# A two-layer diffusion backbone on one core: context-first token groups and a rebuilt entry into the seven-product FFN

## The chip, the cores and the metric

One core of a Trainium2 chip runs the whole network in one launch. The metric is the device time of one execution in microseconds, the median of several runs. Weights come from device memory in every run; nothing is prepared on the device beforehand.

## The reference, cut to what matters

```python
D_MODEL, SEQ, DEPTH, CTX_LEN, D_FF = 1024, 512, 2, 256, 2816

def modulate(t, g, shift, scale):
    return rmsnorm(t, g) * (1.0 + scale) + shift

def ada_mod(cond, w, b):
    m = jax.nn.silu(cond) @ w + b
...
def swiglu(h, w_up, w_down):
    a, b = jnp.split(h @ w_up, 2, axis=-1)
    return (jax.nn.silu(a) * b) @ w_down

def ffn_sublayer(t, mod, i, g, w_up, w_down):
    h = modulate(t, g, mod[3 * i], mod[3 * i + 1])
    return t + 0.5 * mod[3 * i + 2] * swiglu(h, w_up, w_down)
...
def merge_branches(o_a, o_b, g_logits, b_gate, w_pa, w_pb, w_o):
    g_a, g_b = jnp.split(jax.nn.sigmoid(g_logits + b_gate), 2, axis=-1)
    return (g_a * (o_a @ w_pa) + g_b * (o_b @ w_pb)) @ w_o
```

Each of the two layers is a half-step FFN, a token mixing (neighbourhood attention and a gating MLP, merged by gates and projected), and a second half-step FFN. All run over 512 latent and 256 context tokens with the same weights; the second FFN of layer 1 needs the latent tokens alone. Everything is in fp32.

## The kernel before

Activations lie transposed: a tile is 128 channels (partitions) by up to 768 tokens, the latent ones at columns 0 to 511, the context ones at 512 to 767. The residual stream is eight tiles `x`, the input of a stage eight tiles `h`. An fp32 product is made of three fp32r matmuls: every weight and every activation is split into a high part (`hi`, `hh`, `gh`, a rounding cast on ACT) and a remainder (`lo`, `hl`, `gl`, the difference), and PE does hi·hi, hi·lo and lo·hi (L464, L465, L467 for ordinary blocks). One block is 128 output channels: 8 (or fewer) k steps of three matmuls for each token group, gathered in one of eight PSUM banks per group.

**Weights** pass through `Stream` in one fixed order: SP issues the DMA into one of five raw buffers (`wraw`), ACT casts the high part (L253), and GpSimd (POOL) subtracts the remainder (L254); there are nine `wq` tiles for the parts, and a `Unit` of 1024 columns takes two. The raw buffer is free again when the remainder has been made.

**Order.** Tasks are listed up front (`task`), each a generator; while its matmuls are issued, every step advances the weight stream and one step of the background generators (`side`, `side2`, the deferred `tail`). So the order on every engine is fixed when the program is built, and each engine runs its list in order. `extras` puts units of the conditioning product between tasks (ada units: 512 KB raw, two DVE products 128x1024 each, L552); `require` forces those that a stage needs.

**FFN** (`ffn`). The up-projection has 22 pairs of 128 channels (a and b). In the three FFNs that have both token sets (both of layer 0 and the first of layer 1) the first pairs are standard blocks (`up`, and `opening`, which takes the first three blocks one token group after the other), `STANDARD` = four in the very first FFN (the start FFN), two in the later ones. The other pairs go through `up_pair`: seven products of 384 columns (L779 to L781) instead of eight, on sums and differences of quarters of h and of the weights. The operands of h (`t42`, `t3`, `t1`) are made by `combine` from whole h, which POOL restores as hh + hl (tile `hb`, L728), by four subtractions on DVE (L721) and rounding on ACT with a difference on DVE (L746, L747), for each of four k. Then `settle` writes `t1` over the right halves of hh and hl, so no standard block may follow it. `act` makes silu(a)·b for a standard pair (ACT L890, DVE L891) and splits the product into gh (ACT L795) and gl (DVE L796). The quarters of the weights are sums and differences on DVE (L287), with cast and remainder on ACT and DVE. The down-projection runs in parts of four pairs (`MAINS`), between groups of up pairs, with residuals on DVE (L805).

**Between stages.** `close` does the last down (or output) products with the residual, and in its background, for one token group after the other: squares (ACT L619, POOL L626), sums by PE (L635), statistics (L655), the reciprocal root spread over the partitions (L669), and the `norm` of the next stage: per tile `nu` on DVE (L693), hh on ACT (L697), hl on DVE (L706), the latter two with the shift added. Into the later seven-product FFNs the two groups are `EVEN`, 384 and 384 columns.

**Mixing** ends with `gates` (2 x 8 units of 1024), `merge` (8 units of 1024) and `project` (8 of 640), each followed by extras, and then `close`.

## Time and profile before

| | us |
|---|---|
| median of three runs | 3045.46 (3044.94 to 3045.81) |
| profiled execution, its own time | 3043.34 |
| its span in the trace | 3041.5 |
| PE busy | 2919.8 |
| DVE busy | 1804.1 |
| ACT busy | 1112.0 |
| POOL busy | 1069.5 |

The page gives the busy time of each engine over the span. The table of waits says for each engine at which line it stood and what released it. A timeline lists single instructions with start and duration; a bracket gives the idle time in front and what ended it. The granted clock of TensorE is 1.00 or 0.50 of full speed in a short window (2.4 or 1.2 GHz).

### The profile page before, as it was taken

To read this page: it belongs to the slowest core of one execution; us is meant where nothing else is said; L and a number is where in the kernel's file an instruction comes from. 1 tells how busy PE (TensorE), PEld (TensorE's weight loads), DVE (VectorE), ACT (ScalarE), POOL (GpSimd) and SP (SyncE) were. 2 spreads that over 40 slices of the span, in tenths; PEclk is the share of its full clock that TensorE was granted. 3 is DMA by queue.
4 is the path that set the end of the run, shared out by engine and by line. 5 is a ranking of instruction groups with operands and counts; after the bars stand their busy time and mean duration, and the time that the engine had idled before them with its cause. 6 is when DMAs were issued, how large, how long until landed. Compare 5 with 4: busy or idle time off the path is not lost. (4 is left out here: it accounts for less than half of the span.)

```text
span 3041.5 us, 42332 instructions
## 1 busy us (share of the span) xinstructions
PE 2919.8 (96%) x16316; PEld 2652.7 (87%) x16316; DVE 1804.1 (59%) x3075; ACT 1112.0 (37%) x2033; POOL 1069.5 (35%) x760
## 2 busy tenths in 40 slices
PE   8899999999999997999999889999999999999998
PEld 5789999889998887999999789999989887888887
DVE  5787766645566748756766876766564646421113
ACT  4233334334552233334333343333343643332222
POOL 2322222354444343222123422222246545544443
PEclk9899999999999998999999899999999999999999
DMA  6233322242223230322233022333224334332231
GB/s 232 86 114 108 108 91 86 95 153 70 80 87 125 93 113 24 118 86 91 87 111 118 15 75 100 110 122 115 77 93 161 105 101 155 122 97 94 87 97 63
DMA packets 103353, 309.13 MB, mean 102 GB/s; under 512 B 13040, under 2 KB 15344, under 8 KB 103152
## 3 DMA queue, kind: packets, MB, share of 16 engines
q1 hardware_dynamic: 100160, 294.70, 29.2%
q0 software_dynamic: 2560, 11.54, 1.0%
q8 instruction: 128, 2.10, 0.3%
q14 instruction: 73, 0.60, 0.1%
q10 hardware_dynamic: 432, 0.20, 0.0%
HBM read 286.46 MB, written 8.39 MB: 97 GB/s over the span
## 5 line engine op out<-in xcount | busy, mean ns | idle before, releaser
L254 POOL TENSOR_TENSOR wq<-wraw,wq 128x512 fp32r<-128x512 f32 (+2 forms) x454 | 804.9, 1780 | 1645.3 <-ACT wq L253 1379.4
L253 ACT CAST wq<-wraw 128x512 fp32r<-128x512 f32 (+2 forms) x686 | 480.8, 722 | 610.2 <-DMA wraw<-dm 220.7
L464 PE MATMUL ps<-hh,wq 128*128 128x512 f32 (+2 forms) x1344 | 489.3, 364 | 6.1 <-ACT hh L697 6.1
L465 PE MATMUL ps<-hl,wq 128*128 128x512 f32 (+2 forms) x1344 | 470.3, 359 | 1.9 <-DVE hl L706 1.8
L467 PE MATMUL ps<-hh,wq 128*128 128x512 f32 (+2 forms) x1344 | 433.4, 358 | 0.2 <-POOL wq L254 0.2
L464 PE MATMUL ps<-gh,wq 128*128 128x512 f32 (+2 forms) x1248 | 430.8, 345 | 1.9 <-ACT wq L253 1.9
L465 PE MATMUL ps<-gl,wq 128*128 128x512 f32 (+2 forms) x1248 | 406.2, 343 | 0.0
L805 DVE SCALAR_TENSOR_TENSOR x<-ps,mods,x 128x512 f32<-128x512 f32 (+3 forms) x416 | 238.1, 602 | 283.0 <-PE ps L467 282.7
L467 PE MATMUL ps<-gh,wq 128*128 128x512 f32 (+2 forms) x1248 | 350.6, 344 | 0.4 <-POOL wq L254 0.4
L552 DVE SCALAR_TENSOR_TENSOR products<-wraw,condb 128x1024 bf16<-128x1024 f32 x224 | 328.3, 1466 | 2.9 <-DMA wraw<-ada 1.1
L464 PEld LDWEIGHTS ps<-hh,wq 128*128 128x128 f32 x1344 | 256.5, 191 | 56.0 <-ACT hh L697 7.4
L465 PEld LDWEIGHTS ps<-hl,wq 128*128 128x128 f32 x1344 | 256.9, 191 | 38.0 <-DVE hl L706 4.0
L464 PEld LDWEIGHTS ps<-gh,wq 128*128 128x128 f32 x1248 | 235.1, 188 | 54.0 <-ACT wq L253 2.2
L465 PEld LDWEIGHTS ps<-gl,wq 128*128 128x128 f32 x1248 | 235.2, 188 | 28.4
L467 PEld LDWEIGHTS ps<-hh,wq 128*128 128x128 f32 x1344 | 237.3, 192 | 22.7 <-POOL wq L254 0.6
L254 DVE TENSOR_TENSOR wq<-wraw,wq 128x512 fp32r<-128x512 f32 x232 | 179.7, 775 | 64.2 <-ACT wq L253 64.2
L467 PEld LDWEIGHTS ps<-gh,wq 128*128 128x128 f32 x1248 | 202.8, 190 | 8.2 <-POOL wq L254 0.6
L779 PE MATMUL px<-t42h,wq 128*128 128x384 f32 x464 | 159.2, 343 | 14.2 <-ACT ce L908 12.0
L1229 PE MATMUL ps<-wq,hh 128*128 128x256 f32 x704 | 165.2, 329 | 0.0
L779 PE MATMUL pz<-hh,wq 128*128 128x384 f32 x464 | 157.8, 340 | 4.2 <-ACT ce L908 4.2
L781 PE MATMUL px<-t42h,wq 128*128 128x384 f32 x464 | 158.6, 342 | 2.7 <-DVE wq L254 2.7
L780 PE MATMUL px<-t42l,wq 128*128 128x384 f32 x464 | 158.6, 342 | 0.0
(209 smaller groups left out, 5514.9 us busy)
## 6 DMA issues: line engine op xcount, KB each, us to landing
wraw<-up SPq DMA_DIRECT2D x176, 512.0 KB, 3.3
wraw<-ada SPq DMA_DIRECT2D x128, 512.0 KB, 3.3
wraw<-dm SPq DMA_DIRECT2D x160, 256.0 KB, 2.7
wraw<-win SPq DMA_DIRECT2D x72, 512.0 KB, 3.3
wraw<-pab SPq DMA_DIRECT2D x16, 512.0 KB, 3.2
ch<-first SPq DMA_DIRECT2D x16, 384.0 KB, 8.2
xs<-x POOLq DMA_DIRECT2D x16, 384.0 KB, 5.8
bt<-bt SPq DMA_DIRECT2D x16, 384.0 KB, 3.2
```

The source lines that it names most:

```text
L253: self.nc.scalar.copy(out=hi, in_=src)
L254: eng.tensor_tensor(out=lo, in0=src, in1=hi.bitcast(F32), op=ALU.subtract)
L464: nc.tensor.matmul(out[g][:, :n], lhsT=wh, rhs=xh[:, o:o + n], start=first, stop=False)
L465: nc.tensor.matmul(out[g][:, :n], lhsT=wh, rhs=xl[:, o:o + n], start=False, stop=False)
L467: nc.tensor.matmul(out[g][:, :n], lhsT=wl, rhs=xh[:, o:o + n], start=False, stop=last)
L552: nc.vector.scalar_tensor_tensor(out=self.products, in0=unit.raw, scalar=1.0, in1=self.condb[c], op0=ALU.mult, op1=ALU.mult, accum_out=m[: ...
L779: nc.tensor.matmul(ps[:, :H], lhsT=wh, rhs=xh, start=first and k == 0, stop=False, skip_group_check=True)
L780: nc.tensor.matmul(ps[:, :H], lhsT=wh, rhs=xl, start=False, stop=False, skip_group_check=True)
L781: nc.tensor.matmul(ps[:, :H], lhsT=wl, rhs=xh, start=False, stop=last and k == KQ - 1, skip_group_check=True)
L805: self.nc.vector.scalar_tensor_tensor(out=self.x[d][:, o:o + n], in0=ps[:, at:at + n], scalar=self.mod(l, idx, d, p), in1=self.x[d][:, o:o ...
L1229: nc.tensor.matmul(ps[:, at:at + 256], lhsT=c(t[k]), rhs=w, start=k == 0 and i == 0, stop=k == KD - 1 and i == 2)
```

## The change

1. `STANDARD` is (4, 3): the two later seven-product FFNs do three standard pairs instead of two.
2. The token groups at every entry into a seven-product FFN are `BOTH` (context 256, then latent 512) instead of `EVEN`, in `close`, `norm` and `opening`.
3. At those entries `norm` writes into tiles `hb` that are kept: ACT adds the shift a second time in place, so the tile holds whole h, and hl is a plain difference of it and hh. `combine` takes these tiles; POOL's additions are gone. In the start FFN, which has no such norm, the additions are made by DVE, one per step. The settling is part of `combine` now, released by a task behind the last standard block.
4. In the start FFN the first down part stands right behind the four standard pairs, ahead of the first seven-product pair, and has no extras in it.
5. The remainders of the standard up units in the two later seven-product FFNs (12 units of 1024) and of gates (32 units of 1024), merge (16 of 1024) and project (16 of 640) of both layers are made by DVE instead of POOL.
6. Numbers of extras: more in the start's up-products and the rest of that FFN, none in the first half of the gates, more behind merge, some behind project.

```diff
@@ -43,11 +43,11 @@
-EXTRAS = (0.65, 0.65, 0.85, 0)
-MIX_EXTRAS = (1, 0.7)
+EXTRAS = (0.85, 0.65, 0.85, 0)
+MIX_EXTRAS = (1, 1, 1)
 QUIET = 5
-START_EXTRAS = 1.2
-STANDARD = (4, 2)
+START_EXTRAS = 1.6
+STANDARD = (4, 3)
...
-EVEN = ((0, H), (H, H))
...
-            self.split(u.raw[:, :u.n], u.hi, u.lo, self.nc.gpsimd)
+            self.split(u.raw[:, :u.n], u.hi, u.lo, getattr(self.nc, u.eng))
...
-                us[d] = self.t3("nu")[:, :n]
+                if whole is None:
+                    us[d] = self.t3("nu")[:, :n]
+                else:
+                    if len(whole) == d:
+                        whole.append(self.t3("hb"))
+                    us[d] = whole[d][:, o:o + n]
...
+                    if whole is not None:
+                        nc.scalar.activation(
+                            out=us[d][:, at:at + m], in_=us[d][:, at:at + m], func=AF.Identity,
+                            bias=self.mod(l, 3 * i, d, p),
+                        )
...
+                    if whole is not None:
+                        nc.vector.tensor_tensor(
+                            out=hl[e][:, a:a + m], in0=us[e][:, at:at + m], in1=hh[e][:, a:a + m].bitcast(F32),
+                            op=ALU.subtract,
+                        )
+                        continue
...
-    def combine(self, h):
+    def combine(self, h, whole):
...
-                b.append(self.t3("hb"))
-                nc.gpsimd.tensor_tensor(out=b[-1], in0=hh[d].bitcast(F32), in1=hl[d].bitcast(F32), op=ALU.add)
-            yield
+                if whole:
+                    b.append(whole[d])
+                    whole[d] = None
+                else:
+                    b.append(self.t3("hb"))
+                    nc.vector.tensor_tensor(out=b[-1], in0=hh[d].bitcast(F32), in1=hl[d].bitcast(F32), op=ALU.add)
+                    yield
...
+        while not self.may_settle:
+            yield
+        for k in range(KQ):
+            u = t["t1"].pop(0)
+            self.parted(u[:, :H], hh[k][:, H:], hl[k][:, H:])
+            u = None
+            yield
+        self.settled = True
...
-    def settle(self, h):
-
-        while self.side2:
-            self.step()
-        for k, u in enumerate(self.t["t1"]):
-            self.parted(u[:, :H], h[0][k][:, H:], h[1][k][:, H:])
-        self.t["t1"] = None
...
+        eng = "vector" if seven and not start else "gpsimd"
         j0 = STANDARD[not start] if seven else NF
-        ups = [[Unit(A["up"][(base * NF + j) * 2 + s], 1024) for s in range(2)] if j < j0 else
+        ups = [[Unit(A["up"][(base * NF + j) * 2 + s], 1024, eng=eng) for s in range(2)] if j < j0 else
...
-                if j == j0:
-                    self.settle(h)
+                while not self.settled:
+                    self.step()
...
-                if p < len(MAINS) - 1 or d < QUIET:
+                if (p > 0 or not start) and (p < len(MAINS) - 1 or d < QUIET):
                     self.extras(EXTRAS[base])
...
-            while j <= f0 + m if p < len(MAINS) - 1 else j < NF:
+            ahead = f0 + m + (not start or p > 0)
+            while j < ahead if p < len(MAINS) - 1 else j < NF:
                 (up_pair(j) if j >= j0 else up(j)) if j else begin() if start else first()
                 j += 1
+                if j == j0:
+                    self.task([], free)
...
-            for s, un in enumerate((unit(20 + d), unit(28 + d))):
+            for s in range(2):
+                un = Unit(win[20 + 8 * s + d], 1024, eng="vector")
...
-                self.extras(MIX_EXTRAS[0])
+                if d >= KD // 2:
+                    self.extras(MIX_EXTRAS[0])
...
-            un = Unit(A["pab"][l * KD + d], 1024)
+            un = Unit(A["pab"][l * KD + d], 1024, eng="vector")
...
-            un = Unit(A["om"][l * KD + d], (KD - O_LAST) * P)
+            un = Unit(A["om"][l * KD + d], (KD - O_LAST) * P, eng="vector")
...
             self.task([un], gen)
+            self.extras(MIX_EXTRAS[2])
...
-                core.ffn(l, 0, (LAT, CTX), hbox, EVEN, BOTH, box, then(l, 1, BOTH), start=l == 0)
+                core.ffn(l, 0, (LAT, CTX), hbox, BOTH, BOTH, box, then(l, 1, BOTH), start=l == 0)
```

In layer 0 the mixing and the second FFN get their groups in the same way. The order of the instructions moves in three places. In it L717 is the hl of the norm, L739 the subtractions (L721 before), L750 the additions, L780 the differences (L747), L830 the residual (L805), L917 the multiplication (L891), L821 the gl (L796), L253 the remainder (L254), L286 the quarters (L287).

DVE at the entry into the seven products in the second FFN of layer 0, before: the norm's end, the first weight quarters, the combine's first steps.

```order
L706 SCALAR_TENSOR_TENSOR hl<-nu,mods_106,hh 128x256
L287 TENSOR_TENSOR s_10674<-wraw 128x512
L287 TENSOR_TENSOR wraw<-wraw 128x512
L254 TENSOR_TENSOR wq<-wraw,wq 128x512
L287 TENSOR_TENSOR wraw<-wraw 128x512
L721 TENSOR_TENSOR hb<-hb 128x384 x4
L747 TENSOR_TENSOR t42l<-hb,t42h 128x768
L747 TENSOR_TENSOR t3l<-hb,t3h 128x384
L721 TENSOR_TENSOR hb<-hb 128x384 x4
```

DVE at the same place, after: the norm's end, a remainder, the combine's first two steps.

```order
L698 SCALAR_TENSOR_TENSOR hb<-x,mods_106,rs 128x512
L717 TENSOR_TENSOR hl<-hb,hh 128x512 x2
L253 TENSOR_TENSOR wq<-wraw,wq 128x1024
L739 TENSOR_TENSOR hb<-hb 128x384 x4
L780 TENSOR_TENSOR t42l<-hb,t42h 128x768
L780 TENSOR_TENSOR t3l<-hb,t3h 128x384
L739 TENSOR_TENSOR hb<-hb 128x384 x4
L780 TENSOR_TENSOR t42l<-hb,t42h 128x768
```

The quarters of the first seven-product weights have left this place, and one remainder of a whole unit has come. At the combine's end in the kernel before:

```order
L747 TENSOR_TENSOR t42l<-hb,t42h 128x768
L747 TENSOR_TENSOR t3l<-hb,t3h 128x384
L891 TENSOR_TENSOR s<-s,ps 128x384 x2
L796 TENSOR_TENSOR gl<-s,gh 128x768
L254 TENSOR_TENSOR wq<-wraw,wq 128x512 x2
L287 TENSOR_TENSOR wraw<-wraw 128x512
```

And after:

```order
L780 TENSOR_TENSOR t42l<-hb,t42h 128x768
L780 TENSOR_TENSOR t3l<-hb,t3h 128x384
L917 TENSOR_TENSOR s<-s,ps 128x512
L917 TENSOR_TENSOR s<-s,ps 128x256
L821 TENSOR_TENSOR gl<-s,gh 128x768
L253 TENSOR_TENSOR wq<-wraw,wq 128x1024 x2
L286 TENSOR_TENSOR s_10896<-wraw 128x512
L286 TENSOR_TENSOR wraw<-wraw 128x512
```

The remainders behind the first multiplication are those of a standard unit, the quarters come later.

DVE at the transition from the mixing of layer 0 into that FFN, before: residuals of the closing projection (L805), between them pieces of the first group's norm, then the statistics of the second.

```order
L805 SCALAR_TENSOR_TENSOR x<-ps,mods_106,x 128x128
L805 SCALAR_TENSOR_TENSOR x<-ps,mods_106,x 128x256
L693 SCALAR_TENSOR_TENSOR nu<-x,mods_106,rs 128x384
L706 SCALAR_TENSOR_TENSOR hl<-nu,mods_106,hh 128x384
L693 SCALAR_TENSOR_TENSOR nu<-x,mods_106,rs 128x384
L706 SCALAR_TENSOR_TENSOR hl<-nu,mods_106,hh 128x384
L805 SCALAR_TENSOR_TENSOR x<-ps,mods_106,x 128x128
L805 SCALAR_TENSOR_TENSOR x<-ps,mods_106,x 128x256
L693 SCALAR_TENSOR_TENSOR nu<-x,mods_106,rs 128x384
L706 SCALAR_TENSOR_TENSOR hl<-nu,mods_106,hh 128x384 x2
L658 TENSOR_SCALAR nw<-st 128x3
```

And after:

```order
L698 SCALAR_TENSOR_TENSOR hb<-x,mods_106,rs 128x256
L717 TENSOR_TENSOR hl<-hb,hh 128x256
L253 TENSOR_TENSOR wq<-wraw,wq 128x1024
L830 SCALAR_TENSOR_TENSOR x<-ps,mods_106,x 128x512
L698 SCALAR_TENSOR_TENSOR hb<-x,mods_106,rs 128x256
L717 TENSOR_TENSOR hl<-hb,hh 128x256
L698 SCALAR_TENSOR_TENSOR hb<-x,mods_106,rs 128x256
L717 TENSOR_TENSOR hl<-hb,hh 128x256
L830 SCALAR_TENSOR_TENSOR x<-ps,mods_106,x 128x512
L698 SCALAR_TENSOR_TENSOR hb<-x,mods_106,rs 128x256
L717 TENSOR_TENSOR hl<-hb,hh 128x256 x2
L658 TENSOR_SCALAR nw<-st 128x4
```

The pieces have 256 columns, and a remainder on DVE stands among them.

DVE in the start FFN up to the multiplication of the fourth standard pair (L891) and the first settling row (hl), before the change:

```order
L254 TENSOR_TENSOR wq<-wraw,wq 128x512
L287 TENSOR_TENSOR wraw<-wraw 128x512
L254 TENSOR_TENSOR wq<-wraw,wq 128x512 x2
L287 TENSOR_TENSOR wraw<-wraw 128x512
L552 SCALAR_TENSOR_TENSOR products,mods_106<-wraw,condb_640 128x1024
L552 SCALAR_TENSOR_TENSOR products,mods_106<-wraw,condb_641 128x1024
L254 TENSOR_TENSOR wq<-s_940,wq 128x512
L254 TENSOR_TENSOR wq<-wraw,wq 128x512
L891 TENSOR_TENSOR s<-s,ps 128x512
L891 TENSOR_TENSOR s<-s,ps 128x256
L796 TENSOR_TENSOR gl<-s,gh 128x768
L747 TENSOR_TENSOR hl<-hb,hh 128x384 x4
```

And after, up to the same multiplication (L917):

```order
L552 SCALAR_TENSOR_TENSOR products,mods_106<-wraw,condb_640 128x1024
L750 TENSOR_TENSOR hb<-hh,hl 128x768
L552 SCALAR_TENSOR_TENSOR products,mods_106<-wraw,condb_641 128x1024
L739 TENSOR_TENSOR hb<-hb 128x384 x4
L780 TENSOR_TENSOR t42l<-hb,t42h 128x768
L780 TENSOR_TENSOR t3l<-hb,t3h 128x384
L552 SCALAR_TENSOR_TENSOR products,mods_106<-wraw,condb_640 128x1024
L552 SCALAR_TENSOR_TENSOR products,mods_106<-wraw,condb_641 128x1024
L552 SCALAR_TENSOR_TENSOR products,mods_106<-wraw,condb_640 128x1024
L917 TENSOR_TENSOR s<-s,ps 128x512
L917 TENSOR_TENSOR s<-s,ps 128x256
L821 TENSOR_TENSOR gl<-s,gh 128x768
```

The multiplication of the fourth pair now has no weight quarters in front of it but the additions; the first seven-product pair is not on the queue yet. On PE, behind the last standard block of the start FFN, stood:

```order
L465 MATMUL ps<-hl,wq 128x256
L467 MATMUL ps<-hh,wq 128x512
L467 MATMUL ps<-hh,wq 128x256
L779 MATMUL px<-hh,wq 128x384
L780 MATMUL px<-hl,wq 128x384
```

And now the first down part:

```order
L465 MATMUL ps<-hl,wq 128x256
L467 MATMUL ps<-hh,wq 128x512
L467 MATMUL ps<-hh,wq 128x256
L464 MATMUL ps<-gh,wq 128x512
L465 MATMUL ps<-gl,wq 128x512
```

The seven products' first operand is needed later, the gh and gl of the standard pairs earlier.

## Rows read from the trace of the kernel before

**Rows 1.** From the page of the kernel before: busy time of each engine, its share of the span and its instructions.

```profile
PE 2919.8 (96%) x16316; PEld 2652.7 (87%) x16316; DVE 1804.1 (59%) x3075; ACT 1112.0 (37%) x2033; POOL 1069.5 (35%) x760
```

**Rows 2.** The waits of PE over the whole span: the line that waits, the engine and tile waited for, then the total in us, the number of waits and the longest.

```profile
PE px L779 <- ACT s L890: 23.0, 2, 11.7
PE ss L635 <- ACT sq L619: 18.9, 9, 6.5
PE px L779 <- ACT ce L908: 12.0, 3, 5.2
```

**Rows 3.** Windows of the trace: the window in us from the span's start, its length, the busy time (and instructions) of PE, PEld, DVE, ACT and POOL, the granted clock of TensorE as a share of full speed, the DMA share and GB/s. The first two cover the start FFN from its last standard up-products to a steady pace; the other three are stretches at half clock, two in the start FFN and one at the entry into the second FFN of layer 0.

```profile
100.00:160.00 60.00, 44.09 (x211) 39.44 (x210) 49.22 (x76) 17.21 (x32) 12.31 (x8) 0.83 0.27 93
160.00:210.00 50.00, 47.33 (x267) 43.76 (x267) 41.67 (x65) 16.52 (x31) 12.50 (x9) 1.00 0.35 127
113.63:123.87 10.24, 6.10 (x19) 5.59 (x20) 10.02 (x15) 3.34 (x7) 1.82 (x1) 0.50 0.15 51
127.29:134.11 6.82, 3.90 (x12) 3.90 (x13) 6.47 (x9) 3.48 (x8) 2.43 (x2) 0.50 0.31 111
1185.42:1199.07 13.65, 4.58 (x14) 4.58 (x15) 9.82 (x16) 7.80 (x13) 1.08 (x1) 0.50 0.00 1
```

**Rows 4.** Timeline of PE inside a standard up-block of the start FFN, at full clock: start in us, duration, instruction. The distance from one start to the next is the pace.

```profile
67.07 0.40 PE L465 MATMUL ps<-hl,wq 128*128 128x512 f32 x1
67.31 0.28 PE L464 MATMUL ps<-hh,wq 128*128 128x256 f32 x1
67.42 0.28 PE L465 MATMUL ps<-hl,wq 128*128 128x256 f32 x1
```

**Rows 5.** Timelines at the transition from the mixing of layer 0 into its second FFN, and, in the last two rows, at the one from there into layer 1: PE (the last two products of the closing projection, the last sum of squares, the first product of the opening), DVE, POOL, PE again. In brackets the idle time before an instruction and what ended it.

```profile
1132.94 0.33 PE L465 MATMUL ps<-ml,wq 128*128 128x384 f32 x1
1133.12 0.34 PE L467 MATMUL ps<-mh,wq 128*128 128x384 f32 x1
1141.25 1.49 PE L635 MATMUL ss<-sq,ones 128*32 128x384 f32 x2 [3.90 <-ACT sq L619]
1147.61 0.67 PE L464 MATMUL ps<-hh,wq 128*128 128x384 f32 x1
1136.30 2.58 DVE L706 SCALAR_TENSOR_TENSOR hl<-nu,mods,hh 128x384 fp32r<-128x384 f32 x1
1139.85 0.73 DVE L805 SCALAR_TENSOR_TENSOR x<-ps,mods,x 128x128 f32<-128x128 f32 x2
1136.12 2.35 POOL L254 TENSOR_TENSOR wq<-wraw,wq 128x1024 fp32r<-128x1024 f32 x1 [1.33 <-ACT wq L253]
1691.49 0.34 PE L467 MATMUL ps<-gh,wq 128*128 128x384 f32 x1
1706.64 0.67 PE L464 MATMUL ps<-hh,wq 128*128 128x384 f32 x1
```

**Rows 6.** Timelines of the entry into the seven products in the second FFN of layer 0: POOL, DVE, PE.

```profile
1161.38 17.79 POOL L728 TENSOR_TENSOR hb<-hh,hl 128x768 f32<-128x768 f32 x8
1166.39 8.55 DVE L721 TENSOR_TENSOR hb<-hb 128x384 f32<-128x384 f32 x4
1184.20 2.40 DVE L721 TENSOR_TENSOR hb<-hb 128x384 f32<-128x384 f32 x4
1188.90 2.40 DVE L721 TENSOR_TENSOR hb<-hb 128x384 f32<-128x384 f32 x4
1194.49 0.69 PE L779 MATMUL px<-hh,wq 128*128 128x384 f32 x1 [11.66 <-ACT s L890]
1195.30 0.52 PE L781 MATMUL px<-hh,wq 128*128 128x384 f32 x1
1195.62 0.52 PE L779 MATMUL px<-hh,wq 128*128 128x384 f32 x1
```

**Rows 7.** Timelines of the start FFN while the operands of the seven products are made: POOL, DVE.

```profile
93.93 7.88 POOL L728 TENSOR_TENSOR hb<-hh,hl 128x768 f32<-128x768 f32 x4
69.95 2.40 DVE L721 TENSOR_TENSOR hb<-hb 128x384 f32<-128x384 f32 x4
95.81 7.02 DVE L721 TENSOR_TENSOR hb<-hb 128x384 f32<-128x384 f32 x4 [4.10 <-POOL hb L728]
109.86 1.01 DVE L891 TENSOR_TENSOR s<-s,ps 128x512 f32<-128x512 f32 x2
111.77 0.96 DVE L796 TENSOR_TENSOR gl<-s,gh 128x768 fp32r<-128x768 f32 x1 [0.90 <-ACT gh L795]
```

**Rows 8.** Windows (columns as in Rows 3) in the mixing of layer 0: attention's second part and the gates, the merge, the projection up to its closing part.

```profile
856.00:1000.00 144.00, 140.14 (x815) 122.45 (x814) 94.42 (x159) 57.13 (x92) 61.93 (x46) 1.00 0.33 116
1000.00:1067.00 67.00, 66.34 (x379) 57.68 (x378) 50.60 (x70) 12.91 (x17) 20.00 (x10) 1.00 0.28 94
1067.00:1118.00 51.00, 51.00 (x294) 46.04 (x293) 19.21 (x28) 12.28 (x18) 25.09 (x19) 1.00 0.42 146
```

**Rows 9.** Groups of equal instructions over the whole span: line, engine, operation, tiles, shapes, number | busy us, mean ns of one | idle time before them.

```profile
L254 POOL TENSOR_TENSOR wq<-wraw,wq 128x1024 fp32r<-128x1024 f32 x162 | 404.3, 2500 | 481.1 <-ACT wq L253 351.8 <-PE ps L467 87.2 <-PE ps L465 21.6
L254 DVE TENSOR_TENSOR wq<-wraw,wq 128x512 fp32r<-128x512 f32 x232 | 179.7, 775 | 64.2 <-ACT wq L253 64.2
L552 DVE SCALAR_TENSOR_TENSOR products<-wraw,condb 128x1024 bf16<-128x1024 f32 x224 | 328.3, 1466 | 2.9 <-DMA wraw<-ada 1.1
L706 DVE SCALAR_TENSOR_TENSOR hl<-nu,mods,hh 128x512 fp32r<-128x512 f32 x24 | 18.0, 750 | 3.8 <-ACT hh L697 3.3
```

37 lines of the change are left out of this document (22 added, 15 removed).

## The prediction

> **What bounds the kernel now.** The busy times come first [rows 1]: PE is busy for 96% of the span, DVE for 59%, POOL for 35%. So most of the time is the number of matmuls at their pace, and a change of order can win only PE's idle time and the half-clock stretches behind it. Second, the table of waits says where that idle time lies [rows 2]: 23.0 us in two waits of the first seven-product pair for the Silu of the first standard pair, 18.9 for the squares of a closing residual, 12.0 for the first copy out of the seven products. Third, the windows size the start [rows 3]: in 100 to 160 us PE is busy for 44.09 of 60, in 160 to 210 for 47.33 of 50. Fourth, the timelines show who is late at each of these places [rows 5 to 7]. Every place is the same story: DVE makes the operands of the seven products, or ends a norm, and PE stands.
>
> The pace gives prices. Starts at 67.07, 67.31 and 67.42 are 0.24 us after a 512-column product and 0.11 after a 256-column one [rows 4], 0.35 for the two; two 384-column products start 0.18 apart at full clock (1132.94, 1133.12, [rows 5]) and 0.32 apart at half clock (1195.30, 1195.62, [rows 6]), so each product at half clock loses 0.14 to 0.15 us.
>
> **Part 1, one more standard pair in each of the two later FFNs.** A standard pair is 2 blocks x 8 x 3 x 0.35 = 16.6 us (0.345 from longer chains), a seven-product pair 84 x 0.175 = 14.7. Two are exchanged: **+3.8 us** of plain PE work. Groups of 256 and 512 instead of 384 and 384 cost 0.35 against 0.35: nothing.
>
> **Part 2, the entry into the seven products (twice).** Before, the combine waits for POOL: eight adds take 17.79 us from 1161.38, and the first four subtractions beside them 8.55 us, where four alone take 2.40 [rows 6]. From then on a step of the combine is 4.7 us (1184.20 to 1188.90, ACT's rounding included). It ends near 1193.7, the Silu follows, and PE starts at 1194.49 after 11.66 us idle; 14 products run at half clock [rows 3], 2.1 us, and the wait for the copy comes next (two of the three in [rows 2]: 12.0 less the longest, 5.2, so 3.4 each), with the restart's tail 1 to 2 more. I count 18.9 us for the first entry and 17.1 for the second.
>
> The Trainium skill, page "SBUF — State Buffer", section "Who interferes with whom", says that a DVE instruction with two SBUF inputs contends with a GpSimd instruction that reads SBUF. The 8.55 against 2.40 us agrees.
>
> After, the norm keeps whole h on ACT's time (one more pass per tile), so the eight POOL adds are gone and no add replaces them. From the opening's first product: the norm of 512 columns, 2 us until its first tile and then 8 x 2 x 0.75 [rows 9], 14; a remainder now on DVE, two times 0.68 to 0.775 [rows 9], taken as 1.3; four steps of 4.7: 34.1 us. PE's cover is the opening's three blocks and the one behind, 72 x 0.118 + 72 x 0.227 + 24 x 0.345 = 33.1 us, about what it was before. But the third standard pair needs PSUM banks that the first pair's multiplication (DVE, 1.01, [rows 7]) frees, and weights whose cast and remainder are queued on ACT and DVE behind that multiplication, the gh round and the gl subtraction (0.90 + 0.96, [rows 7]) and one more remainder: 34.1 + 1.0 + 1.9 + 1.3 = 38.3, so 5.5 us idle, then 2.5 of half clock and 1 for the copy behind the settling rounds: 9 us. Both places: 9.9 + 8.1, **-18**. Bounds: no stall at all (-36) if the weights' casts slip ahead; -4 if DVE is as slow there as beside POOL's adds.
>
> **Part 3, the transitions (twice).** The last product of the closing projection is at 1133.12, the first of the opening at 1147.61: 14.3 us idle; in the next one 1691.49 to 1706.64, 15.0 [rows 5]. Of the 14.3, 6.7 pass until DVE reaches the last residual at 1139.85, behind norm pieces of the first token group; one of these took 2.58 us beside a POOL remainder of 2.35. After, the first group has 256 columns instead of 384 and hl is a plain subtraction, so each queued piece is about two thirds as long, and the remainder is on DVE, thus not beside it but before it (1.3). The chain behind (squares, sum at 1141.25, statistics, rs, hh) stays: 7.8 us. I take 6.7 -> 2 in layer 0's, a little less, 15.0 -> 11.5, in the other, of which only the ends are shown, and 0.8 less at half clock: **-9**. Bounds -4 (512 columns in the second group's squares lengthen the chain) and -14 (no backlog).
>
> **Part 4, the start.** Before: 60 - 44.09 + 50 - 47.33 = 18.6 us idle, and 31 products at half clock in the two windows shown, 4.6: 23.2 [rows 3]. POOL's adds hold the subtractions here too (7.02 against 2.40, after 4.10 idle, [rows 7]). After, the eight adds stand on DVE, each priced as a subtraction of the same size, 0.96 [rows 7]. PE gets the first down products when the last standard block ends, near 109; three of the four operands are ready by then, the fourth not. DVE's queue from 69.95 [rows 7] up to the fourth's gl: 8 adds 7.7, four groups of subtractions 9.6, four pairs of t42l and t3l 6.0, three activations of 2.9 each 8.6, eleven ada products at 1.3 (1.466 is the mean beside POOL, [rows 9]) 14.3, some 2 of waits for ACT: 118 without POOL, 123 with two of its remainders (2.50 each, [rows 9]) in the way. PE wants it at 109 + 3 x 1.04 = 112. Stall 6 to 11, taken as 11, plus 4 for the half clock and for weights that come late: the down part's loads (and the ada units', eight in the up-products instead of six) now stand ahead of the first pair's on SP's queue; the DMA share is 0.27 there [rows 3], so bandwidth is free, but a raw buffer is held until DVE has done its ada product. In all 15. **-8**, bounds -17 (118 and no half clock) and +2 (every ada product and add beside POOL, 4 x 4.6 more). Behind the down products (8 x 4 x 1.04 = 33 us of PE work) the combine and the settling are over, so the idle places of the first seven-product pair are covered.
>
> **Part 5, remainders on DVE in gates, merge and project, and the shifted extras.** 48 units of 1024 at 2 x 0.775 and 16 of 640 at 0.97 make 90 us of DVE work [rows 9]; POOL loses 48 x 2.5. It hides if DVE has room: gates of layer 0, 94.42 of 144 us plus 16 x 1.55, less 8 ada units of 2.9 that go, leave 48 free; merge, 50.60 + 8 x 1.55 + 2.4 units of 2.9 = 70 of 67: at its bound; projection, 19.21 + 8 x 0.97 + 8 x 2.9 = 50 of 51 [rows 8]. The remainder is the lo operand of a block, so where DVE is full PE waits; but alone it takes 0.68 and POOL gets out of its way. I take **+1**, bounds -8 (the remainder comes 1 us sooner than POOL's 2.5 where PE waits for it) and +6 (both merges at their bound). The other extras only change place.
>
> **Sum.** +3.8 - 18 - 9 - 8 + 1 = -30. The profiled execution took 3043.3 us (span 3041.5), so 3013; the median is 2.1 above that execution: 3015.
>
> **Rivals.** *One, the entry's wait only moves.* If the weights behind the first activation on ACT and DVE come as late as the seven products' operands did, the third standard pair waits as long as the first seven-product pair does now. For it: in the new order that multiplication still stands behind the whole combine. Against it: the combine starts 8 to 10 us sooner without POOL's adds. Part 2 gives nothing: 3033.
>
> *Two, slower: the remainders in gates and merge reach PE's path.* DVE runs in order, so a remainder waits behind residuals and ada products. From 31 us of the 90 exposed (0.5 of each of the 64 units) the gain is eaten, from 37.5 (0.6 of each) the kernel is slower than 3051.5. With half of it exposed, 45, in place of the 1 in the sum: 3059. For it: layer 0's merge has no room left. Against it: the gates have.
>
> *Three, no difference: exchanging work between POOL and DVE gives nothing.* DVE has in the start the adds that it waited for before, so part 4 is 0, and a fifth of the 90 us shows in the merges, 18: 3015 + 8 + 18 = 3041. For it: the subtractions that are slow beside POOL [rows 6, 7] show that the two engines get in each other's way, and POOL keeps its other remainders. Against it: at the entries the adds go away altogether.
>
> The Trainium skill, page "Perfetto Trace Analysis", section "Optimizing Scalar/DVE Operations", speaks for this: the two share an SBUF read port, "so offloading operations between those two might not help". By that rule 3041; the trace bears out the sharing, not yet the conclusion.
>
> **How the numbers follow.** The measurement can tell about 0.2%, 6 us: faster is below 3039.4, slower above 3051.5. Forecast 0.66 (its own range 2990 to 3032 from the bounds of the parts, which will not all fall on one side), rival one 0.16, rival three 0.08, rival two 0.10. The first two are faster: 0.82; the third the same: 0.08; the second slower: 0.10. The range 2988 to 3041 holds the forecast's, rival one's and rival three's time; beyond it lie rival two and the outer bounds, together 2 in 10.
>
> **What would show it.** Entry: four subtractions of 2.4 us, no POOL work beside them, first Silu within 36 us of the opening, idle 4 to 7 us before the third standard pair. Transition: last residual 2 to 3 us after the last product, 9 to 10 us idle. Start: one wait of 6 to 12 us in the first down block, for gh or gl. Mixing: windows as full as before. Wrong would be idle PE before the third operand in merge or gates, a later entry, or a start stall over 20 us.

## Result and the profile after

The changed kernel takes 3004.68 us (median of 4 runs, 3003.51 to 3010.05) against 3045.64 us (median of 4 runs): a ratio of 0.9869, with a 95% interval from 0.9852 to 0.9886. That is 41 us less, where 30 were forecast; the time lies inside the forecast's own range. The profiled execution was the slowest of its four, 3010.05 us with a span of 3007.9, 33.6 below the span before. In a second profile of the same kernel (run e9 below) the span is 3004.3.

The page after, line of busy times, to be held against [rows 1]:

```profile
PE 2924.7 (97%) x16340; PEld 2635.0 (88%) x16340; DVE 1784.2 (59%) x3087; ACT 1120.2 (37%) x2033; POOL 846.4 (28%) x660
```

PE is busy for 4.9 us more, POOL for 223 us less, DVE for 20 less although it has taken over remainders. The waits of PE, to be held against [rows 2]; L635 is the sum of squares, L464 the first matmul of an ordinary block:

```profile
PE ss L635 <- ACT sq L619: 14.8, 5, 6.5
PE ps L464 <- ACT wq L252: 7.4, 3, 3.8
PE ps L464 <- ACT gh L820: 3.0, 1, 3.0
```

The two waits of 11 us for the Silu and the waits for the first copy have left the list; what stands there now is a wait of a standard block for its weights (7.4 us in three places, 3.8 of it in the start). The squares still cost 14.8.

Where the time went is read best by stage. The table adds up, over all matmuls of a stage in the trace, the time from one start to the next less the full-clock pace of its shape (0.227 us for 512 columns, 0.174 for 384, 0.118 for 256): idle time, half clock and the slow first products behind a wait together. A transition runs from 25 us before the second `rs` (L669) to 3 us behind it, an entry is the 72 us behind that; "start" is 60 to 200 us; the bodies are what lies between. Stages that are not listed changed by -1.1 us in all; they are in the last row.

| us over the pace | before | after | after, again (e9) | change | forecast |
|---|---|---|---|---|---|
| start | 30.3 | 16.7 | 16.6 | -13.6 | -8 |
| rest of the first FFN, layer 0 | 4.7 | 14.5 | 14.6 | +9.8 | 0 |
| mixing, layer 0 | 40.8 | 40.2 | 38.7 | -0.6 | +1, both |
| transition into the second FFN, layer 0 | 12.5 | 13.1 | 13.1 | +0.6 | -5.5 |
| entry there | 20.3 | 5.6 | 5.9 | -14.7 | -9.9 |
| rest of that FFN | 11.6 | 6.9 | 7.0 | -4.7 | 0 |
| transition into layer 1 | 13.8 | 14.9 | 13.8 | +1.1 | -3.5 |
| entry there | 18.7 | 5.8 | 4.4 | -12.9 | -8.1 |
| mixing, layer 1 | 41.9 | 41.5 | 41.4 | -0.4 | with the above |
| all stages | 230.5 | 194.0 | 190.6 | -36.5 | |

Counted in the traces, the changed kernel has 408 more products of 512 columns, 408 more of 256 and 792 fewer of 384: 3.0 us more of plain work at these paces. With them the table gives -33.5, and the two spans differ by 33.6. The second profile shows how far one execution repeats: within 0.3 us in most stages, 1.1 to 1.5 in three of them.

**The entry.** DVE, ACT and PE at the entry in layer 0, to be held against [rows 6]:

```profile
1158.53 2.33 DVE L739 TENSOR_TENSOR hb<-hb 128x384 f32<-128x384 f32 x4
1172.26 2.33 DVE L739 TENSOR_TENSOR hb<-hb 128x384 f32<-128x384 f32 x4
1177.24 0.87 ACT L916 ACTIVATE s<-ps 128x512 f32<-128x512 f32 x2
1179.67 2.51 ACT L252 CAST wq<-wraw 128x1024 fp32r<-128x1024 f32 x3
1180.76 0.50 PE L464 MATMUL ps<-hh,wq 128*128 128x512 f32 x1 [1.91 <-ACT wq L252]
```

Four subtractions take 2.33 us in each step, in the first too, where it was 8.55, and POOL does nothing from the transition to 1189 us. The Silu starts 33.6 us behind the opening's first product (1143.69). In front of that Silu ACT spends 1.28 us on a table load (ACT_TABLE_LOAD at 1175.95), which the forecast left out. PE waits 1.91 us for one cast, before the third standard pair, and 1.48 in e9.

**The transition**, to be held against [rows 5]: PE's last product of the closing projection, ACT's cast of a standard unit, its remainder on DVE and the last two residuals, then PE's last sum of squares and the first product of the opening.

```profile
1127.53 0.39 PE L467 MATMUL ps<-mh,wq 128*128 128x512 f32 x1
1129.62 1.03 ACT L252 CAST wq<-wraw 128x1024 fp32r<-128x1024 f32 x1
1130.68 1.23 DVE L253 TENSOR_TENSOR wq<-wraw,wq 128x1024 fp32r<-128x1024 f32 x1 [1.21 <-ACT wq L252]
1131.82 0.75 DVE L830 SCALAR_TENSOR_TENSOR x<-ps,mods,x 128x512 f32<-128x512 f32 x1
1134.55 0.74 DVE L830 SCALAR_TENSOR_TENSOR x<-ps,mods,x 128x512 f32<-128x512 f32 x1
1136.01 1.91 PE L635 MATMUL ss<-sq,ones 128*32 128x512 f32 x2 [0.97 <-DVE hl L717]
1143.69 0.56 PE L464 MATMUL ps<-hh,wq 128*128 128x256 f32 x1
```

From the last product to the last residual it is 7.0 us as it was 6.7; from that residual to the opening 9.1, was 7.8; in all 16.2, was 14.5.

**The start** (the end of an ada product and the third pair's multiplication on DVE, the gh rounding and the cast of weights on ACT, PE twice, a remainder on POOL, PE in the down part), to be held against [rows 7]:

```profile
99.08 0.08 DVE L552 DVE_READ_ACCUMULATOR products<-wraw,condb 128x1 f32 x1
99.08 1.01 DVE L917 TENSOR_TENSOR s<-s,ps 128x512 f32<-128x512 f32 x2
100.12 0.83 ACT L820 CAST gh<-s 128x768 fp32r<-128x768 f32 x1 [8.66 <-DVE s L917]
102.01 1.04 ACT L252 CAST wq<-wraw 128x1024 fp32r<-128x1024 f32 x1
103.10 0.79 PE L464 MATMUL ps<-hh,wq 128*128 128x512 f32 x1 [3.80 <-ACT wq L252]
106.67 1.01 PE L467 MATMUL ps<-hh,wq 128*128 128x512 f32 x2 [1.92 <-POOL wq L253]
103.18 3.44 POOL L253 TENSOR_TENSOR wq<-wraw,wq 128x1024 fp32r<-128x1024 f32 x1 [19.12 <-ACT wq L252]
122.09 0.50 PE L464 MATMUL ps<-gh,wq 128*128 128x512 f32 x1 [3.00 <-ACT gh L820]
```

and three windows, the transition's and the two of the start, to be held against [rows 3]:

```profile
1130.00:1150.00 20.00, 13.86 (x61) 10.14 (x61) 11.07 (x24) 10.38 (x19) 0.00 (x0) 0.66 0.08 26
100.00:160.00 60.00, 51.36 (x267) 44.36 (x268) 54.22 (x76) 18.19 (x32) 19.26 (x11) 0.91 0.35 114
160.00:210.00 50.00, 50.00 (x286) 50.00 (x285) 30.22 (x49) 23.44 (x45) 9.84 (x7) 1.00 0.15 54
```

PE stands in the fourth standard pair (3.80 and 1.92) and before the fourth operand of the down part (3.00). The cast that it waits for first stands on ACT behind the gh rounding of the third pair, and that waits for the multiplication, which DVE does behind an ada product. Within 100 to 160 us these waits make 8.6 us of idle time (60 - 51.36), the only ones up to 210 us, where 18.6 stood before; the clock averages 0.91 in the first window instead of 0.83.

**The first FFN's rest.** The window 200 to 480 us, before and after:

```profile
200.00:480.00 280.00, 280.00 (x1597) 267.17 (x1596) 195.46 (x299) 98.05 (x185) 65.66 (x49) 1.00 0.30 99
```

```profile
200.00:480.00 280.00, 273.88 (x1540) 258.08 (x1539) 191.28 (x300) 89.48 (x168) 64.88 (x45) 0.99 0.29 102
```

Before, PE is busy for all 280 us, afterwards 273.88, while DVE is busy for 191.28, 4 us less than before. One of the places, DVE with an ada product (L552), the quarters of a weight pair (L286) and the sum `ce` (L932), and PE:

```profile
368.54 1.21 DVE L552 SCALAR_TENSOR_TENSOR products<-wraw,condb 128x1024 bf16<-128x1024 f32 x1
370.29 1.79 DVE L286 TENSOR_TENSOR s<-wraw 128x512 f32<-128x512 f32 x1
374.05 0.55 DVE L932 TENSOR_TENSOR ce<-px,ce 128x384 f32<-128x384 f32 x1
374.65 0.44 PE L804 MATMUL px<-t42h,wq 128*128 128x384 f32 x1 [2.15 <-DVE ce L932]
```

`ce` stands in DVE's queue behind ada products and quarters that are not needed yet.

**Mixing of layer 0**, windows shifted by 4 us, to be held against [rows 8]:

```profile
852.00:996.00 144.00, 141.96 (x817) 123.99 (x816) 75.56 (x142) 57.77 (x94) 18.74 (x31) 0.99 0.25 87
996.00:1063.00 67.00, 67.00 (x384) 58.51 (x383) 57.22 (x91) 13.07 (x15) 3.86 (x7) 1.00 0.45 155
1063.00:1114.00 51.00, 51.00 (x312) 44.73 (x312) 44.80 (x75) 13.32 (x21) 11.76 (x8) 1.00 0.55 179
```

DVE has 57.22 of 67 us in the merge where 70 were forecast, 75.56 of 144 before it where 96 were, 44.80 of 51 behind it where 50 were. PE does not wait in the merge or the projection.

### The profile page after: what moved, and what is told of

The parts are those of the page before. It is cut to its first block, busy times and chain, and to the rows that moved or that the text cites. A ratio compares the mean times of both kernels' runs of the same rounds, so it can differ in the third digit from the quotient of the medians.

```text
span 3007.9 us, 42173 instructions
## 1 busy us (share of the span) xinstructions
PE 2924.7 (97%) x16340; PEld 2635.0 (88%) x16340; DVE 1784.2 (59%) x3087; ACT 1120.2 (37%) x2033; POOL 846.4 (28%) x660
## 3 DMA queue, kind: packets, MB, share of 16 engines
q0 software_dynamic: 2560, 11.54, 1.0%
## 5 line engine op out<-in xcount | busy, mean ns | idle before, releaser
L253 POOL TENSOR_TENSOR wq<-wraw,wq 128x512 fp32r<-128x512 f32 (+1 forms) x378 | 639.6, 1700 | 1527.9 <-ACT wq L252 1294.2
L464 PE MATMUL ps<-hh,wq 128*128 128x512 f32 (+1 forms) x1408 | 512.9, 364 | 12.7 <-ACT wq L252 7.4
L465 PE MATMUL ps<-hl,wq 128*128 128x512 f32 (+1 forms) x1408 | 490.9, 359 | 1.9 <-DVE hl L722 1.8
L467 PE MATMUL ps<-hh,wq 128*128 128x512 f32 (+1 forms) x1408 | 451.9, 359 | 2.5 <-POOL wq L253 2.1
L464 PE MATMUL ps<-gh,wq 128*128 128x512 f32 (+1 forms) x1248 | 430.8, 345 | 3.1 <-ACT gh L820 3.0
L465 PE MATMUL ps<-gl,wq 128*128 128x512 f32 (+1 forms) x1248 | 406.6, 343 | 0.5 <-DVE gl L821 0.5
L830 DVE SCALAR_TENSOR_TENSOR x<-ps,mods,x 128x256 f32<-128x256 f32 (+1 forms) x400 | 234.8, 618 | 239.8 <-PE ps L467 239.7
L467 PE MATMUL ps<-gh,wq 128*128 128x512 f32 (+1 forms) x1248 | 350.6, 343 | 0.0
L253 DVE TENSOR_TENSOR wq<-wraw,wq 128x512 fp32r<-128x512 f32 (+2 forms) x300 | 253.6, 846 | 162.2 <-ACT wq L252 156.3
L464 PEld LDWEIGHTS ps<-hh,wq 128*128 128x128 f32 x1408 | 270.3, 192 | 69.5 <-ACT wq L252 8.4
L552 DVE SCALAR_TENSOR_TENSOR products<-wraw,condb 128x1024 bf16<-128x1024 f32 x224 | 311.0, 1389 | 1.6
L465 PEld LDWEIGHTS ps<-hl,wq 128*128 128x128 f32 x1408 | 270.3, 192 | 42.1 <-DVE hl L722 3.9
L464 PEld LDWEIGHTS ps<-gh,wq 128*128 128x128 f32 x1248 | 235.1, 188 | 55.8 <-ACT gh L820 3.3
L467 PEld LDWEIGHTS ps<-hh,wq 128*128 128x128 f32 x1408 | 247.4, 193 | 27.8 <-POOL wq L253 2.8
L805 PE MATMUL px<-t42l,wq 128*128 128x384 f32 x448 | 152.1, 339 | 0.0
```

Of the source, the lines that this page charges most:

```text
L253: eng.tensor_tensor(out=lo, in0=src, in1=hi.bitcast(F32), op=ALU.subtract)
L464: nc.tensor.matmul(out[g][:, :n], lhsT=wh, rhs=xh[:, o:o + n], start=first, stop=False)
L465: nc.tensor.matmul(out[g][:, :n], lhsT=wh, rhs=xl[:, o:o + n], start=False, stop=False)
L467: nc.tensor.matmul(out[g][:, :n], lhsT=wl, rhs=xh[:, o:o + n], start=False, stop=last)
L552: nc.vector.scalar_tensor_tensor(out=self.products, in0=unit.raw, scalar=1.0, in1=self.condb[c], op0=ALU.mult, op1=ALU.mult, accum_out=m[: ...
L805: nc.tensor.matmul(ps[:, :H], lhsT=wh, rhs=xl, start=False, stop=False, skip_group_check=True)
```

## Experiments

Each run but e9, e11 and e12 undoes or alters one thing in the changed kernel. Ratios are to the kernel before on the same chip; e1 to e4, e5 to e8 and e9 to e12 ran on three chips, so medians are compared within such a group and ratios across them. Single executions lie up to 10 us apart, so the stage in the trace decides, and the median tells what is left of it. In the stages the second profile of the changed kernel is the one to compare with where the two differ.

| run | median us | ratio, 95% interval | stages against the changed kernel |
|---|---|---|---|
| e1 two standard pairs | 3013.4 | 0.9891 (0.9877 to 0.9904) | entries 9.8 and 10.4 |
| e2 additions on POOL | 3023.2 | 0.9924 (0.9912 to 0.9937) | entries 14.4 and 15.7, transitions 11.5 and 13.7 |
| e3 groups 384 and 384 | 3014.4 | 0.9898 (0.9883 to 0.9914) | transitions 15.4 and 16.3, entries 6.8 and 7.2 |
| e4 0.70 extras | 3005.9 | 0.9868 (0.9854 to 0.9881) | first FFN 5.6, second 11.9, third 11.6 (was 9.6) |
| e5 standard units on POOL | 3011.0 | 0.9879 (0.9866 to 0.9893) | transitions 10.5 and 12.3, entries 9.1 and 8.8 |
| e6 mixing on POOL | 3004.9 | 0.9855 (0.9839 to 0.9871) | mixing 37.8 and 35.0 |
| e7 down part late | 3028.8 | 0.9939 (0.9926 to 0.9951) | start 35.5 |
| e8 start's additions on POOL | 3015.2 | 0.9890 (0.9874 to 0.9905) | start 23.2 |
| e9 changed kernel again | 3007.1 | 0.9872 (0.9858 to 0.9887) | table above |
| e10 opening's units on POOL | 3004.9 | 0.9866 (0.9849 to 0.9882) | transitions 9.6 and 13.3, entries 5.9 and 5.4 |
| e11 and mixing on POOL | 3003.9 | 0.9860 (0.9845 to 0.9874) | mixing 45.2 and 37.6 |
| e12 and 0.70 extras | 3000.5 | 0.9848 (0.9833 to 0.9862) | first FFN 5.6, second 13.1 |

**e1, two standard pairs.**

```diff
-STANDARD = (4, 3)
+STANDARD = (4, 2)
```

> The changed kernel with two standard pairs instead of three in the two later seven-product FFNs; all else as changed (3004.7 us). Theory 'POOL's additions': the entry became short because the combine no longer waits for them, and PE's cover up to the first pair's Silu is the same three opening blocks and one more whatever STANDARD is. Then PE waits 3 to 5 us at each first seven-product pair instead of 1.9 at the third standard pair, plain work falls by 3.8 us: 3002 to 3007. Theory 'cover': the third pair's 16.6 us hide the combine; then each entry loses 8 to 12 us again: 3017 to 3025.

```profile
PE px L804 <- ACT ce L934: 9.2, 2, 4.6
PE px L804 <- ACT s L916: 2.7, 2, 1.7
```

Between the two: each entry is 4 to 6 us longer, less 1.9 of plain work. At the first seven-product pair PE waits up to 1.7 us for the Silu, where it was 11.7, and 4.6 for the first copy, which stands behind the settling rounds on ACT. So the third pair hides little of the combine, against the theory of the cover; what it hides is mostly the settling and that copy.

**e2, the additions on POOL.**

```diff
-                b.append(whole[d])
...
+                nc.gpsimd.tensor_tensor(out=b[-1], in0=hh[d].bitcast(F32), in1=hl[d].bitcast(F32), op=ALU.add)
```

> The changed kernel with whole h restored by POOL again at the two later entries (no second ACT pass in the norm, hl with the shift added, eight POOL additions per entry); three standard pairs kept. Theory 'POOL's additions': the four subtractions beside them go back from 2.3 to 6 to 9 us, the combine ends 6 to 10 us later and PE waits that long before the third standard pair, less 1 to 2 us that the transition wins without the ACT pass: 3014 to 3022. Theory 'cover': within 3 us of 3004.7.

PE's waits of a standard block for a cast, seven additions on POOL, the first four subtractions on DVE:

```profile
PE ps L464 <- ACT wq L252: 27.6, 3, 12.0
1152.49 15.62 POOL L750 TENSOR_TENSOR hb<-hh,hl 128x768 f32<-128x768 f32 x7 [4.66 <-DVE hl L722]
1162.11 7.02 DVE L739 TENSOR_TENSOR hb<-hb 128x384 f32<-128x384 f32 x4
```

The subtractions take 7.02 us again and PE waits up to 12.0. The entries cost 9 to 11 us more, the transitions 1.6 and 0 to 1 less, since ACT has no second pass. The theory of POOL's additions stands: they make two thirds of what the entries won, by holding the subtractions back and by stretching them. This median lies just over the range of that theory.

**e3, even groups.**

```diff
-                grps, sgrps = ((LAT, CTX), BOTH) if l == 0 else ((LAT,), HALVES)
+                grps, sgrps = ((LAT, CTX), EVEN) if l == 0 else ((LAT,), HALVES)
...
-                after = then(1, 0, BOTH, True) if l == 0 else core.finish(HALVES, box)
+                after = then(1, 0, EVEN, True) if l == 0 else core.finish(HALVES, box)
```

> The changed kernel with token groups of 384 and 384 at the two later entries, all else as changed. The two transitions did not get shorter although the pieces of the first group's norm did. Theory 'context first helps, and something else took it back': with even groups the transitions get 3 to 5 us longer each: 3011 to 3015. Rival 'context first does nothing there, since what it saves in pieces it loses in the 512-column chain of the second group': 3002 to 3007.

Both transitions are 1.4 to 2.5 us longer, both entries 1 to 3, some 7 us in all; by the ratio it is 8 to 9. Context first does help, with half of what was supposed in the transition, and the trace shows why only half. PE's last product, DVE's last residual and PE's first product of the opening in layer 0 (this kernel is one line longer, so L831 is L830 above):

```profile
1126.93 0.34 PE L468 MATMUL ps<-mh,wq 128*128 128x384 f32 x1
1136.61 0.74 DVE L831 SCALAR_TENSOR_TENSOR x<-ps,mods,x 128x128 f32<-128x128 f32 x2
1144.37 0.67 PE L465 MATMUL ps<-hh,wq 128*128 128x384 f32 x1
```

With even groups the last residual comes 9.7 us behind the last product, with context first 7.0. But the chain behind that residual, up to the opening, takes 7.8 us with a second group of 384 columns, as in the kernel before, and 9.1 with 512. So both the theory and its rival are partly right: of 2.7 us that the pieces save, 1.4 go back in the chain.

**e4, fewer extras in the first FFN.**

```diff
-EXTRAS = (0.85, 0.65, 0.85, 0)
+EXTRAS = (0.70, 0.65, 0.85, 0)
```

> The changed kernel with 0.70 instead of 0.85 extras per down product in the first FFN of layer 0: four to five ada units fewer there, which go to later stages. Theory 'DVE is overfilled there': of the 10 us that the down parts of this FFN lost (waits for ce and wq made by DVE behind ada products), 5 to 9 come back: 2996 to 3000. Rival 'those waits come from the order of the tasks and not from the number of units': within 2 us of 3004.7.

```profile
200.00:480.00 280.00, 279.16 (x1590) 265.99 (x1589) 188.18 (x296) 94.85 (x178) 65.43 (x47) 1.00 0.30 99
```

The first FFN has its 9 us back, and the median has not moved. The second FFN becomes 5 us slower, at one place in the main: at 1222 us PE waits 2.50 us for a cast that stands on ACT behind a gh rounding, and a half-clock stretch of 3.4 follows. The kernel before had such a stall in this FFN at another place (2.62 at 1293 us, for a copy). Both sides of the expectation are partly right: the stage obeys the number, the sum doesn't. At the place of the first FFN that is shown above, DVE's queue has the same order in both runs, yet PE waits 0.84 us instead of 2.15; so it is not the order there, but how far DVE has fallen behind.

**e5, remainders of the standard units on POOL.**

```diff
-        eng = "vector" if seven and not start else "gpsimd"
+        eng = "gpsimd"
```

> The changed kernel with the remainders of the standard up units of the two later seven-product FFNs on POOL again. In the changed trace such a remainder stands on DVE ahead of the last two residuals of the transition and waits 1.2 and 2.3 us for its cast before taking 1.2. Theory 'the remainder on DVE took back what the narrower pieces won': both transitions get 2 to 4 us shorter, the entry changes by under 1: 2997 to 3001. Rival 'the squares' chain and the ACT pass decide': within 2 us of 3004.7.

```profile
PE ps L467 <- POOL wq L253: 5.9, 4, 1.9
```

The transitions are 2.6 and 1.5 to 2.6 us shorter, as the theory said. But the entries are 3 to 4 longer: in layer 0's PE waits 3.19 us for the third pair's cast instead of 1.91, and then 1.89 for POOL's remainder. My "under 1" was wrong; by stages the net is 1 to 3 us more, by the ratio 2 to 3, which the intervals do not tell apart from nothing.

**e6, remainders of the mixing on POOL.**

```diff
-                un = Unit(win[20 + 8 * s + d], 1024, eng="vector")
+                un = Unit(win[20 + 8 * s + d], 1024)
...
-            un = Unit(A["pab"][l * KD + d], 1024, eng="vector")
+            un = Unit(A["pab"][l * KD + d], 1024)
...
-            un = Unit(A["om"][l * KD + d], (KD - O_LAST) * P, eng="vector")
+            un = Unit(A["om"][l * KD + d], (KD - O_LAST) * P)
```

> The changed kernel with the remainders of gates, merge and project on POOL again, extras as changed. Forecast step: 90 us of DVE work hide but for about 1 us. If that holds, 3000 to 3008. Rival 'DVE stands at its bound in the merge of layer 0': 5 to 10 us faster with POOL. Rival 'the earlier remainder helps PE, and POOL beside DVE slows both': 5 to 15 us slower.

The window 2400 to 2560 (mixing of layer 1), of the changed kernel again and of this run:

```profile
2400.00:2560.00 160.00, 154.12 (x710) 132.10 (x710) 91.09 (x165) 65.56 (x105) 16.16 (x29) 0.98 0.34 112
```

```profile
2400.00:2560.00 160.00, 155.55 (x731) 132.93 (x731) 90.47 (x141) 63.79 (x101) 72.84 (x50) 1.00 0.34 115
```

The ratio is 0.9855 against 0.9869 and 0.9872 with DVE, with intervals that overlap. In layer 1 PE is busy for 155.55 of 160 us against 154.12, at a clock of 1.00 against 0.98, and over the stage 6.4 us less are lost; this one execution was 7 us faster than the other three of its kernel. POOL is thus not worse for the mixing, perhaps better.

**e7, the first down part late.**

```diff
-            ahead = f0 + m + (not start or p > 0)
+            ahead = f0 + m + 1
```

> The changed kernel with the first down part of the start FFN behind the first seven-product pair again; additions on DVE as changed. Theory 'the placement made the start's 12 us': the first seven-product pair waits for the combine and the settling again, 8 to 14 us: 3013 to 3019. Rival 'it was the additions leaving POOL': 3004 to 3008.

```profile
122.47 0.69 PE L804 MATMUL px<-hh,wq 128*128 128x384 f32 x1 [4.02 <-ACT wq L252]
126.08 0.69 PE L806 MATMUL px<-hh,wq 128*128 128x384 f32 x1 [2.60 <-DVE wq L253]
134.26 0.69 PE L806 MATMUL py<-hh,wq 128*128 128x384 f32 x1 [2.52 <-DVE wq L253]
```

The first seven-product pair waits for its weights: for a cast (4.02), which stands on ACT behind a gh rounding, and for remainders (2.60, 2.52), which DVE makes behind the combine. The start is 18.9 us longer, more than was expected and more than the 13.6 that the whole change won there: with the additions on DVE this placement is needed.

**e8, the start's additions on POOL.**

```diff
-                    nc.vector.tensor_tensor(out=b[-1], in0=hh[d].bitcast(F32), in1=hl[d].bitcast(F32), op=ALU.add)
+                    nc.gpsimd.tensor_tensor(out=b[-1], in0=hh[d].bitcast(F32), in1=hl[d].bitcast(F32), op=ALU.add)
```

> The changed kernel with the additions of the start FFN's combine on POOL again; the first down part early as changed. Theory 'placement': the combine is hidden by the down products, and DVE without eight additions reaches the fourth pair's multiplication sooner or as late: 3000 to 3007. Rival 'additions': the subtractions wait for POOL as in the kernel before, the fourth operand comes 5 to 10 us later: 3010 to 3015.

```profile
109.23 0.80 PE L464 MATMUL ps<-hh,wq 128*128 128x512 f32 x1 [8.69 <-ACT wq L252]
```

The start is 6.6 us longer: the wait in the fourth standard pair is 8.69 instead of 3.80. The theory that put all on the placement falls for the sum, though not for the place: the fourth operand's wait is 3.07, as it was.

**e9, the changed kernel again.**

> The changed kernel itself once more, beside the next three on one chip, since single executions of one kernel lie up to 10 us apart here. If its stages repeat, the start, the two transitions and the two entries come out within 1 us of the first profile, and the time is 3003 to 3010.

It repeats, by stage within 1.5 us; the expected 1 us is passed at the transition into layer 1 (1.1) and the entry there (1.4).

**e10, the opening's units on POOL, the entry's on DVE.**

```diff
-        ups = [[Unit(A["up"][(base * NF + j) * 2 + s], 1024, eng=eng) for s in range(2)] if j < j0 else
+        ups = [[Unit(A["up"][(base * NF + j) * 2 + s], 1024, eng="gpsimd" if 2 * j + s < 3 else eng) for s in range(2)] if j < j0 else
```

> The changed kernel with the remainders of the opening's three units, which fall into the transition, on POOL, and those of the other three standard units, which fall into the entry, on DVE. With all six on POOL the transitions were 2.6 us shorter each and the entries 3.0 to 3.5 longer. Theory 'the two effects belong to different units': the transitions keep 2 to 2.6 each, the entries stay at the changed kernel's 5.6 and 5.8: 4 to 5 us below the changed kernel. Rival 'one shared cause': the entries lengthen here too, no difference.

The last residuals on DVE and PE's last sum of squares in layer 0's transition:

```profile
1126.07 0.74 DVE L830 SCALAR_TENSOR_TENSOR x<-ps,mods,x 128x512 f32<-128x512 f32 x1
1129.94 0.74 DVE L830 SCALAR_TENSOR_TENSOR x<-ps,mods,x 128x512 f32<-128x512 f32 x1
1131.46 1.04 PE L635 MATMUL ss<-sq,ones 128*32 128x512 f32 x2 [2.53 <-DVE hl L717]
```

The two effects belong to different units: transition 9.6 instead of 13.1 in layer 0, 13.3 instead of 13.8 in the other, entries as in the changed kernel. In all four runs without this remainder (e5 and e10 to e12) layer 0's last residual comes 4.2 to 4.3 us behind the last product instead of 7.0, layer 1's 6.5 instead of 8.1; in layer 1 the chain behind it varies from 7.9 to 9.2, and with it the clock: 9.2 in the first profile of the changed kernel, where the granted clock is 0.50 all through it, 8.2 in e9, where it is 1.00 for 3.4 us of it. The sum of stages is 3.7 lower than in e9, the median 2.3, which the intervals alone would not tell apart.

**e11, and the mixing on POOL; e12, and 0.70 extras.** The edits of e10 and e6, then that of e4 with them.

> As the run before, and the remainders of gates, merge and project on POOL as well. With them on POOL alone the mixing of layer 1 showed 6.5 us less waiting and that of layer 0 2.4 us less in one profile, while the median did not move. If that profile is typical: 8 to 13 us below the changed kernel. If it was one lucky execution: 4 to 5 below, as the run before.

> As the run before, and 0.70 extras in the first FFN of layer 0. Fewer ada units there gave 8.9 us back in that FFN, and the units that moved took 5.0 and 2.0 in the two FFNs behind it. Sum of the parts: 10 to 15 us below the changed kernel, about 2992; if the moved units cost all they gave, as the run before.

Layer 1's mixing keeps 3.4 to 3.8 us; layer 0's is 45.2 in e11's profile and 40.6 in e12's against 38.7, and had been 37.8 in e6's, so whether the mixing as a whole gains is not shown. The median of e11 is 3.3 us below the changed kernel, less than either expectation. The run e12 is the fastest: 3000.5 us, 6.6 below the changed kernel on the same chip, each of its four runs (2997.8 to 3003.6) below each of the changed kernel's four (3006.4 to 3011.8). The two intervals of the ratio overlap by 0.0004. It beats both kernels, by less than the parts promised.

## Why the prediction came out

The forecast of 3015 us held in its sign and, within its range, in its size; but four of its terms are off by 5 to 11 us each. The entries gave 9.6 us more than forecast and the start 5.6, the transitions 10.7 less and the other parts of the FFNs 5.1 less; that the sum is so close is in part luck. Of the signs that the prediction named, those of the transition and the start did not appear, and the entry's idle time was shorter than its 4 to 7 us.

**Part 1, the pairs.** +3.8 forecast, +3.0 counted from the products. Right.

**Part 2, the entries.** The mechanism was right in the main: POOL's additions gone (e2: worth 9 to 11 us each), the Silu within 36 us of the opening (33.6), a short idle before the third standard pair. Mis-sized was what stays behind: 9 us each by forecast, 5.6 and 5.8 by the table (and 39.0 had stood there before, not 36.0). The step that failed is "weights whose cast and remainder are queued behind that multiplication, the gh round and the gl subtraction and one more remainder: 38.3". PE waited only for the cast, which stands on ACT behind gh alone (1179.67); the remainder is the third matmul's and came in time. So PE had the weights 37.1 us behind the opening and not 38.3. And PE's cover was 35.2 us instead of 33.1, in part since the opening starts at half clock (granted 0.50 up to 1147.1). Measured -27.6 for the two, not -18. Rival one (the wait only moves, 3033) fell with the 1.91 us.

**Part 3, the transitions.** The step "6.7 -> 2" failed: 7.0 was measured. The narrower pieces do help (e3: 1.4 to 2.5 us each), but the remainder that I had put "before it (1.3)" takes more than its 1.23 us: DVE stands 1.21 us ahead of it, waiting for a cast that ACT does only behind the norm's second pass (1129.62), and 0.5 to 0.7 at several hl. A second step failed beside it: "The chain behind ... stays: 7.8 us". It takes 9.1, since the second group has 512 columns now (7.8 again in e3); the forecast had this among its bounds only. e10 takes the remainder away and gives 3.5 us in layer 0; e2 takes the second pass away and gives 1.6. So the forecast's -9 became +1.7. In the transition into layer 1 the remainder holds the last residual by 1.5 us; what that is worth (0.5 to 2.6 us by e10 and e5) is not settled, since its profiles differ by more than 1 us on their own.

**Part 4, the start.** After the change 15 us were forecast to remain, and 15.4 do between 95 and 210 us, but that the two agree is luck. The forecast had one wait of 11 us for gh or gl in the first down block, and half clock and late weights behind it. There the wait is 3.00 and 7.1 are lost in all. The other 8.3 stand in the fourth standard pair, ahead of the down part, where the forecast had nothing: its weights' cast comes late, behind a gh rounding that waits in turn for DVE. The size before was missed too: the 23.2 from idle windows and half-clock products left out a third half-clock stretch (154.6 to 158.0) and the slow first products behind each wait; by starts it is 27.8 in the same 100 to 210 us. Placement and engine of the additions work only together (e7 +18.9, e8 +6.6). Rival three's part 0 here fell.

**Part 5, the mixing.** +1 forecast, -1.0 measured and -2.6 in the second profile. The two differ by 1.6 on their own, so all that is shown is that the term is small. The estimate of DVE's load, however, was too high in all three windows (70 against 57.22 in the merge), as it took the mean durations of a DVE that shares its time with POOL: in the merge 17 ada products took 1.217 us each where 10 had taken 1.745. Rival two (3059) fell there. The page "Perfetto Trace Analysis" of the Trainium skill, section "Optimizing Scalar/DVE Operations", warned that such a move might not help; for the mixing e6 agrees with it (a ratio of 0.9855 with POOL, 0.9869 with DVE: no gain), for the start's additions e8 doesn't (6.6 us). The numbers of extras in the start's up-products and in the mixing were altered together with these parts and not undone in a run, so their own share is not shown.

**"The other extras only change place"** was wrong: +9.8 us in the first FFN, and the 4.7 that the second won are gone again in e4 (11.9), so they hang on the same numbers. Neither was argued in the prediction. e4 shows that the number of ada units there decides, through how far DVE falls behind; where such a lag meets a sum that PE waits for was not priced, and no rule for it was found.
